# Value products of two key tiles in one run, the compressed branch's weighted probabilities ahead of its block scores, and the last query tile's finishing pieces spread

## The chip, the core and the metric

The kernel runs on one core of a Trainium2 chip. A time is the device time in microseconds (us) of one execution, and the measure is the median of several executions. A core has five engines that each work their own queue of instructions in order and meet through semaphores: TensorE (PE, matmuls; PEld is its weight load), VectorE (DVE), ScalarE (ACT), GpSimd (POOL) and SyncE (SP, which here only issues DMAs).

## What is computed

One layer of a hybrid decoder on 1024 positions of width 1024. A normalized input goes through one projection; half of its columns feed sparse attention (8 heads of 64, 2 key heads), the other half a recurrence; both are concatenated, projected by w_out, added to the input and normalized. The attention part, which the change touches, is this:

```python
s_cmp = jnp.einsum('bgrsd,bgcd->bgrsc', qh, k_cmp) * SCALE
p_cmp = masked_softmax(s_cmp, cmp_end[None, :] <= pos[:, None])
o_cmp = jnp.einsum('bgrsc,bgcd->bgrsd', p_cmp, v_cmp.astype(f32))
imp = jnp.einsum('bgrsc,cj->bgsj', p_cmp, cmp_to_sel_matrix(n_cmp, n_sel))
...
_, sel_idx = lax.top_k(imp, top_n)            # 8 blocks of 64 keys for each query
...
p_sel = masked_softmax(s_sel, (k_pos <= tq[:, None])[:, :, None])   # over the chosen blocks
o_sel = jnp.einsum('bgrqm,bgqmd->bgrqd', p_sel, v_g.astype(f32))
...
p_win = masked_softmax(s_win, w_mask)         # over a window of 512 keys
o_win = jnp.einsum('bgrqk,bgkd->bgrqd', p_win, vwc.astype(f32))
...
o = g[..., 0:1] * o_cmp + g[..., 1:2] * unblock(o_sel) + g[..., 2:3] * unblock(o_win)
...
return x + mix @ w_out
```

## The kernel before

The program goes through a projection stage, the recurrence woven into it, and from about 650 us the attention stage, which alone the change touches (one instance of its first part, for query tile 5, is done at the end of the projection stage). There the 1024 queries are eight tiles of 128, taken in the order 1, 5, 4, 3, 6, 2, 7, 0. Each tile has two branches: b = 0, the selected blocks, and b = 1, the window. A branch runs over key tiles of 128 (`nk` of them: i + 1 for b = 0, at most 5 for b = 1; 66 in all). The chosen blocks are not gathered; a mask in the second operand `q2` excludes the others.

- `Branch.scores(kt)`: PE makes the scores of one key tile, transposed, into `pst` (two PSUM buffers, one for each key head), ACT takes the exponential into `prob` (L1042, three buffers).
- `Branch.values(kt)`: PE multiplies `prob` with the values into `po`. A key tile gives two matmul instructions of 64 output columns, which run as four passes ("po x4" in the trace). Then POOL adds `prob` into `acc` (L1055), for the sum of the softmax; ACT copies `po` to `pos` after the last key tile.
- `Branch.finish()`: PE transposes `acc` (`pz`, L1067), DVE reduces it to sums (L1069), inverts and weights them (`rr`, L1073), POOL widens `rr` to 512 columns (`wide`, L1077), PE transposes that (`prt`, L1081), DVE applies it to `pos`.
- `compressed()`: the compressed blocks of the tile after this one: scores `pcs`, DVE and ACT the softmax (L909, exponential L910, multiplication by the inverse sum L919), the block scores `sp` (L922) and the choice of 8, the gate-weighted probabilities `pw` (L945, "pc" in the trace as well), their transposes on PE (`pct`, L950), ACT's copy (L953), and PE's product with the compressed values, `poc`.
- `row_max()`: an upper bound of the scores from products `pd` and `ps` on PE and reductions on DVE (`bm`, L982 and L994; `nm`, L1006); PE transposes the result (`pnm`, L1008), DVE writes it into `q2` (L1009), which the scores need.
- `load_w_out()`: eight pieces of w_out, each loaded by SP to `wor` (two buffers, which the `xt` tiles of the output share), split by ACT into `woh` (L1113) and by POOL into the remainder `wol` (L1114). Four are left for the branch of tile 5, b = 0.
- `output()`: w_out's product `pout` for a finished query tile, in pieces of three matmuls.

PE's order is fixed by the order of the code. DVE, ACT, POOL and SP are ordered by a scheduler that simulates the program, and then work their queues in that order. `run` walks a branch's key tiles and lets a `Side` object emit pieces of other generators at set fractions of the branch; `side.at` places the finishing pieces of the branch before, at steps 1.2, 1.6 and 3.0 of `nk`, and at 0.95 at the latest. `late_values` keeps the value products one key tile behind the scores.

## Time and profile before

| what | value |
|---|---|
| median of three executions | 1052.12 us (1043.89 to 1053.36) |
| profiled execution, its span | 1040.26 us, 1038.5 us |
| busy PE, PEld, DVE, ACT, POOL | 930.2, 658.6, 584.0, 335.5, 448.2 us |
| mean granted TensorE clock | 0.951 |
| PE busy in 650 to 1039 us, the attention stage | 341.55 of 389 us |

The span goes from the first instruction to the last of the profiled execution; 1.8 us lie around it. The busy times overlap. The granted clock is a share of the full 2.4 GHz; a stretch at 0.5 is one at 1.2 GHz. The last row is the sum of five stretches (80.72, 96.68, 90.73, 45.61 and 27.81 us).

### The profile page before, as it was taken

What the parts mean: (1) busy time and instruction counts of PE and PEld (TensorE: products, weight loads), DVE (VectorE), ACT (ScalarE), POOL (GpSimd) and SP (SyncE); (2) the same over time, 40 slices, a digit from 0 to 9 for tenths busy, and PEclk for the clock granted to TensorE, in tenths of its full rate; (3) what the DMA queues carried; (4) which work ended last, traced back from release to release, by engine and by line L of the source; (5) the groups of instructions that cost most, each with busy time, mean ns of one, the idle gap of its engine ahead of it and who ended that gap; (6) DMA issues with size and microseconds to landing.
All of it is one profiled execution on the core that took longest, in us unless ns stands there. A gap on an engine that the chain in (4) does not pass through costs nothing.

```text
span 1038.5 us, 17087 instructions
## 1 busy us (share of the span) xinstructions
PE 930.2 (90%) x6353; PEld 658.6 (63%) x6353; DVE 584.0 (56%) x1245; ACT 335.5 (32%) x650; POOL 448.2 (43%) x732
## 2 busy tenths in 40 slices
PE   5999999989998999899669978689999999889976
PEld 4888777766676766677458756354565656455555
DVE  7533545555575657374424335677659856685544
ACT  5533233224233443243121212433333333224321
POOL 3100153466483847444521120577463555246521
PEclk9999999999999999799889988879999999899989
DMA  7433453424426453536476293741132312231121
GB/s 259 125 102 102 125 157 108 130 76 116 135 76 172 134 154 119 131 106 170 116 218 192 65 203 95 212 122 31 41 63 79 77 46 69 53 80 33 39 84 41
DMA packets 154429, 115.66 MB, mean 111 GB/s; under 512 B 54369, under 2 KB 132266, under 8 KB 154346
## 3 DMA queue, kind: packets, MB, share of 16 engines
q1 hardware_dynamic: 154346, 114.57, 40.3%
q8 instruction: 50, 0.82, 0.3%
q14 instruction: 33, 0.27, 0.1%
HBM read 76.19 MB, written 35.19 MB: 107 GB/s over the span
## 4 chain that ended last, share of the span: by engine, by line
PE 60%; DVE 10%; DMA 9%; POOL 7%; SPq 6%; issue 5%; ACT 2%; POOLq 0%; DVEq 0%; ACTq 0%
PE pout L113 7%; SPq L85 6%; PE pst L113 6%; PE po L113 5%; PE p_r L113 4%; PE p_k L113 3%; PE p_gn L113 3%; PE p_gr L113 3%; PE p_q L113 3%; PE pc L113 2%; POOL lt L586 2%; POOL ltmp L584 2%; PE ps L113 2%; PE pd L113 2%; PE pcm L113 2%
## 5 line engine op out<-in xcount | busy, mean ns | idle before, releaser
L584 POOL TENSOR_TENSOR ltmp<-la,lt 128x60 f32<-128x60 f32 (+24 forms) x248 | 83.7, 337 | 65.3 <-DMA la<-dA 42.7
L1042 ACT ACTIVATE prob<-pst 128x512 f32<-128x512 f32 x132 | 74.6, 593 | 109.9 <-PE pst L113 106.3
L1055 POOL TENSOR_TENSOR acc<-acc,prob 128x1024 f32<-128x1024 f32 x36 | 86.7, 2409 | 45.1 <-ACT prob L1042 44.9
L586 POOL TENSOR_TENSOR lt<-lt,ltmp 128x60 f32<-128x60 f32 (+24 forms) x248 | 87.6, 353 | 18.8
L113 PE MATMUL pst<-q,k 128*128 128x512 f32 (+1 forms) x264 | 82.3, 430 | 0.0
L994 DVE TENSOR_REDUCE bm<-ps 128x6 f32<-128x384 f32 (+1 forms) x106 | 63.5, 613 | 26.6 <-PE ps L113 26.0
L113 PE MATMUL po<-prob,vt 128*64 128x512 f32 x264 | 75.1, 648 | 0.0
L1055 POOL TENSOR_TENSOR acc<-prob 128x1024 f32<-128x1024 f32 x14 | 33.7, 2410 | 82.6 <-ACT prob L1042 82.6
L113 PEld LDWEIGHTS pst<-q,k 128*128 128x128 f32 (+1 forms) x264 | 48.9, 196 | 14.9 <-issue 5.7
L113 PE MATMUL pout<-woh,mh 128*128 128x512 f32 x128 | 57.6, 450 | 0.2 <-DVE xt L1153 0.2
L113 PE MATMUL ps<-k,q 128*128 128x384 f32 (+3 forms) x136 | 45.4, 386 | 7.7 <-DVE bm L994 3.7
L113 PE MATMUL pout<-wol,mh 128*128 128x512 f32 x128 | 51.3, 401 | 0.0
L113 PE MATMUL pout<-woh,ml 128*128 128x512 f32 x128 | 51.2, 400 | 0.0
L113 PEld LDWEIGHTS ps<-k,q 128*128 128x128 f32 x136 | 25.6, 205 | 35.2 <-DVE bm L994 14.3
L982 DVE TENSOR_REDUCE bm<-pd 128x8 f32<-128x512 f32 x40 | 27.4, 688 | 26.2 <-PE pd L113 26.0
L113 PEld LDWEIGHTS pout<-woh,mh 128*128 128x128 f32 x128 | 25.1, 196 | 20.7 <-issue 17.8
L683 ACT ACTIVATE x<-pc 64x128 f32<-64x128 f32 x32 | 8.7, 272 | 75.4 <-DVE x L682 75.2
L113 PE MATMUL pd<-k,q 128*128 128x128 f32 x160 | 31.1, 321 | 2.1 <-POOL k L868 2.1
L1077 POOL TENSOR_TENSOR wide<-rr,ones 128x512 f32<-128x512 f32 x16 | 17.1, 1068 | 36.1 <-DVE rr L1073 34.1
L1069 DVE TENSOR_REDUCE zz<-pz 128x4 f32<-128x512 f32 x32 | 21.8, 684 | 13.4 <-PE pz L1067 13.0
L1153 DVE TENSOR_TENSOR xt<-pout,xt 128x512 f32<-128x512 f32 x16 | 11.1, 691 | 32.4 <-PE pout L113 32.4
L113 PEld LDWEIGHTS pd<-k,q 128*128 128x128 f32 x160 | 25.9, 204 | 4.0 <-POOL k L868 2.4
(518 smaller groups left out, 2447.7 us busy)
## 6 DMA issues: line engine op xcount, KB each, us to landing
dM<-mix SPq DMA_DIRECT2D x24, 256.0 KB
q<-dQH SPq DMA_DIRECT2D x22, 256.0 KB
la<-dA SPq DMA_DIRECT2D x32, 128.0 KB
xt<-in_x_dram SPq DMA_DIRECT2D x8, 512.0 KB
out_dram<-xt SPq DMA_DIRECT2D x16, 256.0 KB
x<-in_x_dram SPq DMA_DIRECT2D x7, 512.0 KB
mixk<-dM SPq DMA_DIRECT2D x8, 256.0 KB
mixr<-dM SPq DMA_DIRECT2D x8, 256.0 KB
```

The lines of the kernel that those rows point to most:

```text
L85: return nc.sync.dma_start(plain(o), plain(i))
L113: return T.matmul(o, l, r, start=start, stop=stop)
L584: G.tensor_tensor(tv, la[:, j:j + 1, j + 1:].to_broadcast([128, m, n]), lt[:, :m, j:j + 1].to_broadcast([128, m, n]), op=OP.mult)
L586: G.tensor_tensor(lt[:, :m, j + 1:], lt[:, :m, j + 1:], tv, op=OP.add)
L683: gate["A"] = A.activation(x1[1][HP[1], c:8:4, :], pv[HP[1], :, 64:128], AF.Copy)
L982: V.tensor_reduce(bm[:, g * 4:g * 4 + 4, j:j + 2], p.rearrange("p (r b c) -> p r b c", b=2, c=64), axis=AX.X, op=OP.max)
L994: V.tensor_reduce(bm[:, h0:h0 + n, j:j + 2 * w], p[:, :n * w * 128].rearrange("p (h b c) -> p h b c", h=n, c=64), axis=AX.X, op=OP.max)
L1042: A.activation(pr[:, g * 512:(g + 1) * 512], p, AF.Exp)
L1055: G.tensor_tensor(s, self.acc, pr, op=OP.add)
L1069: V.tensor_reduce(zz[:, g, :], p.rearrange("p (r k) -> p r k", r=4), axis=AX.X, op=OP.add)
L1077: G.tensor_tensor(wide, rr.rearrange("p r g -> p (r g)").unsqueeze(2).to_broadcast([128, 8, 64]), ones64.unsqueeze(1).to_broadcast([128, 8 ...
L1153: V.tensor_tensor(xt[:, hs], p, xt[:, hs], op=OP.add)
```

## The change

There are three edits.

1. `run` lets three key tiles' values become pending and then emits two of them in one run; what is left of a branch is emitted after the first scores of the next branch. The 66 value runs on PE become 38: 28 merges. The addition into `acc` moves from `values` to `scores`, so that POOL has it right behind the exponential.
2. In `compressed()` the product `pw` and its transposes `pct` come ahead of the block scores `sp` and the choice of 8 (this concerns tiles 4 to 7 of the queries).
3. For a branch with one key tile (tile 0, the last) the finishing pieces of the branch before come at 0.61, 0.61 and 0.95 of the branch, and the `pout` pieces begin at 0.3 instead of 0.

```diff
@@ compressed
         pw = h2("pc", 2, (128, 4, 2, 64))
         if i >= 4:
             V.tensor_tensor(pe, pe, z8.unsqueeze(2).to_broadcast([128, 8, 64]), op=OP.mult)
+            pg = gv
+        else:
+            pg = sm.tile([128, 8], FT, tag="pg", name="pg")
+            V.tensor_tensor(pg, gv, z8, op=OP.mult)
+        V.tensor_tensor(pw.rearrange("p r g c -> p g r c"), pe.rearrange("p (g r) c -> p g r c", g=2),
+                        pg.rearrange("p (g r) -> p g r", g=2).unsqueeze(3)
+                        .to_broadcast([128, 2, 4, 64]), op=OP.mult)
+        p = psM("pct")
+        for r in range(4):
+            T.transpose(p[:, r * 128:(r + 1) * 128], pw[:, r].rearrange("p g c -> p (g c)"), ident)
+        if i >= 4:
             sp = sm.tile([128, 2, 68], FT, tag="sp", name="sp")
...
-            pg = gv
-        else:
-            pg = sm.tile([128, 8], FT, tag="pg", name="pg")
-            V.tensor_tensor(pg, gv, z8, op=OP.mult)
-        V.tensor_tensor(pw.rearrange("p r g c -> p g r c"), pe.rearrange("p (g r) c -> p g r c", g=2),
-                        pg.rearrange("p (g r) -> p g r", g=2).unsqueeze(3)
-                        .to_broadcast([128, 2, 4, 64]), op=OP.mult)
-        p = psM("pct")
-        for r in range(4):
-            T.transpose(p[:, r * 128:(r + 1) * 128], pw[:, r].rearrange("p g c -> p (g c)"), ident)
         yield
@@ Branch.scores
                 A.activation(pr[:, g * 512:(g + 1) * 512], p, AF.Exp)
+            if kt == 0:
+                self.acc = pr
+            else:
+                s = a2("acc", 2, (128, 1024)) if kt == 1 else self.acc
+                G.tensor_tensor(s, self.acc, pr, op=OP.add)
+                self.acc = s
@@ Branch.values: the same six lines go
@@ the attention stage
+    def flush(keep):
+        while len(late_values) > keep:
+            u, k = late_values.pop(0)
+            u.values(k)
     def run(br, side):
         for kt in range(br.nk):
             br.scores(kt)
+            side.emit((kt + 0.6) / br.nk)
+            if kt == 0:
+                flush(0)
             late_values.append((br, kt))
-            side.emit((kt + 0.6) / br.nk)
-            if len(late_values) > 1:
-                u, k = late_values.pop(0)
-                u.values(k)
+            if len(late_values) == 3:
+                flush(1)
             side.emit((kt + 1) / br.nk)
...
-                    side.at(before.finish(), (1.2, 1.6, 3.0), br.nk)
+                    side.at(before.finish(), (1.2, 1.6, 3.0) if br.nk > 1 else (0.61, 0.61, 0.95), br.nk)
...
-                    side.add(outs[n - 2], 8)
+                    side.add(outs[n - 2], 8, 0.0 if br.nk > 1 else 0.3)
...
-        u, k = late_values.pop(0)
-        u.values(k)
+        flush(0)
```

How the order changes is shown at three places. The first is PE at the first tile, between its window branch and the scores and bounds of what follows; the number behind x counts matmul instructions, two for a key tile's values. The difference, with + for the changed kernel:

```order
 L113 LDWEIGHTS identb
 L113 MATMUL pst<-maskb,identb 128x512
-L113 MATMUL po<-prob,vt_6553 64x512 x2
 L113 MATMUL pst<-q_6524,k_6538 128x512
 L113 MATMUL pst<-q_6529,k_6541 128x512
@@ -2416,5 +2415,5 @@
 L113 MATMUL pd<-k_6532,q_6546 128x128 x4
 L113 MATMUL ps<-k_6532,q_6546 128x512 x3
-L113 MATMUL po<-prob,vt_6553 64x512 x2
+L113 MATMUL po<-prob,vt_6553 64x512 x4
```

The first key tile's value product has moved behind the next scores and stands beside the second's.

The second place is the branch of tile 5, b = 0, where the last four pieces of w_out are split. `prob_7110`, `prob_7145` (7144 after) and `prob_7225` (7226) are its key tiles 1, 2 and 3, `pc_7172` (7173) is the exponential of tile 4's compressed scores, `pc_7264<-pct` the copy of their transposes. ACT before:

```order
L1059 ACTIVATE pos_7089<-po_7036 128x512
L1113 ACTIVATE woh_7342<-wor_7339 128x1024
L1042 ACTIVATE prob_7110<-pst_7111 128x512
L1042 ACTIVATE prob_7110<-pst_7115 128x512
L910 ACTIVATE pc_7172<-pc_7172 128x512
L1113 ACTIVATE woh_7383<-wor_7380 128x1024
L1042 ACTIVATE prob_7145<-pst_7146 128x512
L1042 ACTIVATE prob_7145<-pst_7150 128x512
L1113 ACTIVATE woh_7437<-wor_7434 128x1024
L953 ACTIVATE pc_7264<-pct_7200 128x512
```

And ACT after:

```order
L1114 ACTIVATE woh_7342<-wor_7339 128x1024
L1043 ACTIVATE prob_7060<-pst_7065 128x512
L1114 ACTIVATE woh_7382<-wor_7379 128x1024
L1060 ACTIVATE pos_7089<-po_7084 128x512
L1114 ACTIVATE woh_7439<-wor_7436 128x1024
L1043 ACTIVATE prob_7110<-pst_7111 128x512
L1043 ACTIVATE prob_7110<-pst_7115 128x512
L910 ACTIVATE pc_7173<-pc_7173 128x512
L1114 ACTIVATE woh_7467<-wor_7464 128x1024
L1043 ACTIVATE prob_7144<-pst_7145 128x512
L1043 ACTIVATE prob_7144<-pst_7149 128x512
L954 ACTIVATE pc_7264<-pct_7182 128x512
```

The third of the four pieces (7437 before, 7439 after) has moved from behind key tile 2's exponentials to ahead of key tile 1's. POOL in the same branch before:

```order
L1114 TENSOR_TENSOR wol_7343<-wor_7339,woh_7342 128x1024
L1055 TENSOR_TENSOR acc_7168<-prob_7061,prob_7110 128x1024
L1114 TENSOR_TENSOR wol_7384<-wor_7380,woh_7383 128x1024
L1077 TENSOR_TENSOR wide_7211<-rr_7208,ones64_6514 128x512
L1055 TENSOR_TENSOR acc_7168<-acc_7168,prob_7145 128x1024
L1114 TENSOR_TENSOR wol_7438<-wor_7434,woh_7437 128x1024
```

And POOL after:

```order
L1115 TENSOR_TENSOR wol_7343<-wor_7339,woh_7342 128x1024
L1115 TENSOR_TENSOR wol_7383<-wor_7379,woh_7382 128x1024
L1115 TENSOR_TENSOR wol_7440<-wor_7436,woh_7439 128x1024
L1048 TENSOR_TENSOR acc_7119<-prob_7060,prob_7110 128x1024
L1115 TENSOR_TENSOR wol_7468<-wor_7464,woh_7467 128x1024
L1048 TENSOR_TENSOR acc_7119<-acc_7119,prob_7144 128x1024
L1078 TENSOR_TENSOR wide_7212<-rr_7209,ones64_6514 128x512
```

`wide` stood behind one addition and now stands behind two and the last piece of w_out. In four other branches (tile 5 b = 1, tile 4 b = 1, tile 6 b = 0, tile 7 b = 0) `wide` has likewise moved behind the addition of key tile 2.

The third place is PE at the end, where tile 0's selected branch is finished. Before:

```order
L113 MATMUL pout_9676<-woh_7467,mh_8933 128x512
L113 MATMUL pout_9676<-woh_7467,ml_8934 128x512
L113 MATMUL pout_9676<-wol_7468,mh_8933 128x512
L1067 MATMUL pz_9731<-ident_69,prob_9559 128x128 x4
L1067 MATMUL pz_9737<-ident_69,prob_9559 128x128 x4
L1081 MATMUL prt_9748<-ident_69,wide_9746 128x128 x4
L113 MATMUL po_9756<-prob_9665,vt1_6555 64x512 x2
```

And after:

```order
L1068 MATMUL pz_9695<-ident_69,prob_9560 128x128 x4
L1068 MATMUL pz_9701<-ident_69,prob_9560 128x128 x4
L113 MATMUL pout_9676<-woh_7342,mh_8934 128x512
L113 MATMUL pout_9676<-woh_7342,ml_8935 128x512
L113 MATMUL pout_9676<-wol_7343,mh_8934 128x512
L113 MATMUL pout_9676<-woh_7382,mh_8934 128x512
L113 MATMUL pout_9676<-woh_7382,ml_8935 128x512
L113 MATMUL pout_9676<-wol_7383,mh_8934 128x512
L113 MATMUL pout_9676<-woh_7439,mh_8934 128x512
L113 MATMUL pout_9676<-woh_7439,ml_8935 128x512
L113 MATMUL pout_9676<-wol_7440,mh_8934 128x512
L1082 MATMUL prt_9721<-ident_69,wide_9719 128x128 x4
```

Nine `pout` matmuls now stand between the `pz` transposes and `prt`, and three more behind it, ahead of the value product. At the finish of the branch before (tile 7, b = 1) `pnm` and nine `pout` matmuls stand between `pz` and `prt` in the same way, where nothing stood.

## Rows read from the trace of the kernel before

**Rows 1.** Windows, core 0: us, busy (count) per engine, PE clock, DMA share, GB/s

```profile
960.00:985.00 25.00, 25.00 (x117) 15.18 (x117) 11.88 (x26) 8.62 (x16) 13.38 (x8) 1.00 0.10 32
```

**Rows 2.** The page's chain of work that ended last, by engine

```profile
PE 60%; DVE 10%; DMA 9%; POOL 7%; SPq 6%; issue 5%; ACT 2%; POOLq 0%; DVEq 0%; ACTq 0%
```

**Rows 3.** Windows at a low granted clock, columns as in rows 1

```profile
693.00:701.00 8.00, 5.26 (x17) 3.97 (x19) 7.79 (x19) 2.42 (x4) 5.39 (x3) 0.57 0.40 109
...
885.00:892.00 7.00, 5.75 (x18) 3.53 (x19) 4.12 (x18) 0.60 (x1) 1.04 (x1) 0.51 0.17 65
1001.00:1008.00 7.00, 5.79 (x15) 3.30 (x16) 3.23 (x8) 1.32 (x2) 2.33 (x2) 0.51 0.26 84
```

**Rows 4.** Tile po in 650 to 1039 us: duration ns min/median/max

```profile
L113 PE MATMUL po<-prob,vt x264: 592/643/1117, 651.2 to 1004.2; 128*64 128x512 f32 x132
```

**Rows 5.** Timeline of PE around one value run: start, us, instructions

```profile
863.07 0.40 PE L113 MATMUL ps<-k,q 128*128 128x256 f32 x2
863.40 1.08 PE L113 MATMUL po<-prob,vt 128*64 128x512 f32 x4
864.41 0.50 PE L113 MATMUL pout<-woh,mh 128*128 128x512 f32 x1
864.74 0.39 PE L113 MATMUL pout<-woh,ml 128*128 128x512 f32 x1
864.97 0.39 PE L113 MATMUL pout<-wol,mh 128*128 128x512 f32 x1
```

**Rows 6.** The same run in a narrower window, which cuts its groups

```profile
863.19 0.28 PE L113 MATMUL ps<-k,q 128*128 128x256 f32 x1
863.40 0.65 PE L113 MATMUL po<-prob,vt 128*64 128x512 f32 x2
```

**Rows 7.** Timeline of PE where a value run follows the compressed product

```profile
703.07 1.08 PE L113 MATMUL poc<-pc,vc 64*64 64x512 f32 x4
704.08 1.08 PE L113 MATMUL po<-prob,vt 128*64 128x512 f32 x4
```

**Rows 8.** Timeline at pct of tile 6, and of tile 7; [idle before, releaser]

```profile
788.59 0.63 PE L950 MATMUL pct<-ident,pc 128*128 128x128 f32 x4 [2.15 <-DVE rr L1073]
...
884.58 1.02 DVE L922 TENSOR_REDUCE sp<-pc 128x128 f32<-128x512 f32 x1
...
886.25 1.12 PE L950 MATMUL pct<-ident,pc 128*128 128x128 f32 x4 [4.06 <-DVE pc L945]
```

**Rows 9.** Timeline in tile 5's selected branch, four engines

```profile
685.22 1.08 ACT L1042 ACTIVATE prob<-pst 128x512 f32<-128x512 f32 x2 [1.62 <-PE pst L113]
...
686.07 6.21 SPq L85 DMA_DIRECT2D wor<-in_w_out_dram  x4
...
690.97 1.06 ACT L1113 ACTIVATE woh<-wor 128x1024 fp32r<-128x1024 f32 x1 [0.83 <-DMA wor<-in_w_out_dram]
...
695.74 1.12 PE L950 MATMUL pct<-ident,pc 128*128 128x128 f32 x4 [4.89 <-DVE pc L945]
...
696.97 1.06 PE L1081 MATMUL prt<-ident,wide 128*128 128x128 f32 x4
...
706.82 0.32 PE L1008 MATMUL pnm<-ident,nm 128*104 128x128 f32 x1 [1.67 <-DVE nm L1006]
```

**Rows 10.** Timeline from one set of scores to prt, tile 4's selected branch

```profile
738.18 1.09 PE L113 MATMUL pst<-q,k 128*128 128x512 f32 x4
738.91 1.09 ACT L1042 ACTIVATE prob<-pst 128x512 f32<-128x512 f32 x2 [3.29 <-PE pst L113]
...
740.14 2.37 POOL L1055 TENSOR_TENSOR acc<-acc,prob 128x1024 f32<-128x1024 f32 x1 [2.09 <-ACT prob L1042]
...
743.56 0.66 PE L1081 MATMUL prt<-ident,wide 128*128 128x128 f32 x4 [0.52 <-POOL wide L1077]
```

**Rows 11.** Timeline of PE at the two finishes of the last tile

```profile
988.76 0.66 PE L1081 MATMUL prt<-ident,wide 128*128 128x128 f32 x4 [2.80 <-POOL wide L1077]
...
1002.21 1.12 PE L1081 MATMUL prt<-ident,wide 128*128 128x128 f32 x4 [3.80 <-POOL wide L1077]
```

More of the change, by code (lines that the diff above doesn't have):

```diff
@@ L1050, in values @@
                    pr[:, g * 512:(g + 1) * 512], start=(kt == 0), stop=(kt == self.nk - 1))
-            if kt == 0:
-                self.acc = pr
-            else:
-                s = a2("acc", 2, (128, 1024)) if kt == 1 else self.acc
-                G.tensor_tensor(s, self.acc, pr, op=OP.add)
-                self.acc = s
             if kt == self.nk - 1:
```

## The prediction

> **What bounds the kernel now.** I read the windows of the attention stage first, since the change touches nothing else but one piece of the projection stage. Where the stage runs well, PE is busy without a gap and at the full clock, 25.00 of 25.00 us [rows 1], and the chain of waits that ended last lies on PE for 60% [rows 2]. There, only PE time that is taken away counts. Three other stretches look different: PE is busy only in part, and what it does it does near half speed, at a granted clock of 0.57, 0.51 and 0.51, so mostly at 1.2 of 2.4 GHz [rows 3]. The reader is to see that each of them has a wait of PE in it or ahead of it, 4.89, 4.06 and 3.80 us [rows 8, 9, 11]. There the other engines set the time, and what their queues hold is what counts. So the first edit is priced by PE's steps and the others by waits.
>
> The sum is made against the profiled execution, 1040.26 us. It lies 1.1% under the median of the three, 1052.12 us; the result is scaled by that ratio at the end. The three executions differ by 0.9%, and about 1% (10.5 us) is what a measurement of this kernel can tell from no change.
>
> **Edit 1, value runs.** What a lone run costs is read from matmul starts. The second `ps` starts 0.12 us after the first (863.19 against 863.07), and the run begins 0.21 after it, at 863.40 [rows 5, 6]: 0.09 for the way in. The four passes end at 864.48; the last has at least 0.59 [rows 4], so the second pair began at 863.88, 0.48 after the first. The engine goes on at 864.41, 0.53 after the second pair. The first `pout` matmul then holds it for 0.33 and the second for 0.23 [rows 5]: another 0.10. Together 0.09 + 0.48 + 0.53 + 0.10 = 1.20 us. Two key tiles in one run, if they go on at the step of 0.48, cost 0.09 + 3 x 0.48 + 0.53 + 0.10 = 2.16, which is 0.24 less than 2.40. The nearest row for a boundary inside such a run is the compressed product followed by a value run: 1.01 us from start to start, 0.48 + 0.53 [rows 7], which would save 0.19. 28 merges give 5.3 to 6.7 us. Four lie in tile 5's selected branch, which is priced apart below, and about six of the other 24 end in a wait of PE on DVE or POOL, as the run ahead of `pct` of tile 6 does [rows 8], where PE only comes earlier. 18 x 0.24 = 4.3; I take **-4.2**, with -3.4 (18 x 0.19) and -6.7 (28 x 0.24) as ends.
>
> The trace shows that a second pass follows the first at 0.48 us with its weight load hidden [rows 5, 6]. In a sentence of its own: the Trainium skill, "TensorE: Matmul & The Clock Gate" (section "The mechanism"), says a weight load overlaps running matmuls only where the row group differs; a key tile's values take all rows, so by that the second tile of a run would wait for its loads, and the gain would nearly vanish. By its "TensorEngine Tiling (Array Packing)" (section "Key Properties") only a change of tiling mode drains the engine, which a run of two does once instead of twice. No run here has yet shown two such tiles side by side; the first is rival C.
>
> The merge takes away cover too. A set of scores keeps its two PSUM buffers until the exponentials have read them: the first is free some 0.73 + 0.55 us after the scores start (738.18 to 738.91, and half of 1.09) [rows 10], say 1.3, and the scores themselves take four steps of 0.23, 0.95. So 0.35 us of other work must stand between two sets. Before it was always a value run; now for 28 of them it is only what `Side` has, a `pout` piece of 0.7 us (three steps of 0.23 [rows 5]), which covers it, or a pair of `ps`, 0.24, which doesn't quite. At 0.05 each I take **+1.5**; the ends are 0 and +4 (28 x 0.14).
>
> **The additions in the new place.** Issued behind the exponential, an addition stands earlier in POOL's queue, and in four branches `wide` is now behind that of key tile 2. From scores to `prt` the chain of exponential, addition and `wide` is 743.56 - 738.18 = 5.38 us [rows 10]. Counted from the changed order at the steps of rows 5, PE has 3.6, 4.9, 4.2 and 4.2 us of work of its own between those scores and its `prt`: waits of 1.75, 0.5, 1.2 and 1.2. At 743.56 PE's own work becomes 5.45 and the 0.52 of before goes. Behind the waiting `prt` stands all of PE's queue, so they count in full: **+4.1**. If the merged run stands ahead of the wait, part is cover: 0 as the one end; +4.7 as the other.
>
> **Edit 2.** The reduction of `sp`, 1.02 us, stood between the multiplication and `pw` on DVE [rows 8]; it is now behind. At tile 7 PE waited for just this, 4.06 us: -1.0. At tile 6 PE waited 2.15 us, but the value run ahead of `pct` has gone into a later one, so PE arrives 1.08 us earlier and finds `pct` 1.0 earlier: 0. Tile 5's `pct` lies in the projection stage amid other matmuls: 0. Tile 4's is in the next part. What is late next is the mask: `sp` and the choice of 8 come 0.7 us later (`pw` [rows 8] now precedes them), and `pnm` needs them; it stands far enough behind. **-1.0**, ends 0 and -3.
>
> **Tile 5's selected branch.** Here the queues are dealt anew. ACT's third piece of w_out now stands ahead of key tile 1's exponentials, and before ACT waited for just this piece's load: SP issued it at 686.07, when POOL had freed the buffer, and ACT had it at 690.97, 4.9 us later [rows 9]. The two pieces ahead of it can start some 2 us sooner, so I put the issue at 684, the piece at 689 to 690, and the exponentials at 689.9 instead of 685.22: 4.7 us late. Behind them in ACT's queue are tile 4's exponential and so `pct`; PE's `pct`, which already waited 4.89, comes some 2.5 later even with `sp` out of the way. On POOL the piece and two additions of 2.4 to 2.8 us now precede `wide`: `prt` at about 701.1 instead of 696.97, +4.1. Not all of it stays: further on PE waited 1.67 us for `nm` [rows 9], which DVE can have done in the meantime; with that and four merges (1.0) partly spent, I take **+2.7**. The ends are 0 (the load comes sooner, and the waits of before only change places) and +7.5 (the exponentials' delay in full and a longer stretch at the low clock, of which the one of before cost 5.26 x 0.43 = 2.3 us [rows 3]).
>
> **Edit 3.** Nine `pout` matmuls at 0.23, 2.1 us, go into each of two waits, of 2.80 and 3.80 us [rows 11]. In the first the write of `q2` comes into DVE's queue between the sums: 1.5 stays. In the second, DVE had the addition of the finished `pout` half, its norm and the root between the sums; with the last piece behind `prt` they come later, and 0.4 stays. 6.60 - 1.9 = 4.7. The low clock of 1001 to 1008 costs 5.79 x 0.49 = 2.8 us [rows 3] and followed that wait; a stretch of 0.57 also came where PE had waited only 2.15 [rows 8], so I count on 1.8 of it. **-6.5**; the ends are -3.3 (half of the waits and nothing of the clock) and -7.6.
>
> **The sum**: -4.2 + 1.5 + 4.1 - 1.0 + 2.7 - 6.5 = **-3.4 us**, 1036.9 on the profiled execution, and 1052.12 x 1036.9 / 1040.26 = 1048.7 on the median.
>
> **Rivals.** A, the order holds nobody up: POOL and ACT keep pace in their new orders, the waits at `wide` and in tile 5's branch fill with the merged runs, and the three low stretches go. Then -6.7 (all merges), -2.0 (`pct` of tiles 4 and 7), -5.1 (2.3 + 2.8, clock), -7.6, and +1.5: -19.9 us, or 1032. For it: each low stretch lies at a wait that an edit is aimed at. Against: the changed order puts more of POOL's work ahead of `wide` at five places.
>
> B, slower: in-order queues. ACT's load-bound piece and POOL's additions hold the exponentials and `wide`, and PE's whole queue behind them; the value runs that filled such gaps are gone. +7.5, +4.7, +4.0, one more low stretch +2.5, against -3.4 and -3.3: +12.0 us, or 1064.3. It decides from the point where these waits, which I price at 8.3, exceed the 11.7 us that the other terms give. For it: ACT already waited 0.83 us for that load, and POOL was busy nearly without a pause there. Against: most of the four `wide` waits have over 4 us of matmuls ahead of them.
>
> C, the merge doesn't do what it says: each key tile in a run pays for its own loads, 0.10 [rows 5] ahead of each of two pairs, so that 0.04 of 0.24 is left. Edit 1 gives -0.7 instead of -4.2: +0.1 us, 1052.2. For it: no row shows two key tiles in one run. Against: the 1.01 of rows 7.
>
> **How the numbers follow.** The forecast has 0.46, A 0.25, B 0.16, C 0.13. The forecast's own range, from the ends of its terms that can hold together, is 1041 to 1056. Faster by over 1% (under 1041.6) is most of A and a tail of the forecast: 0.27. Slower by over 1% (above 1062.6) is two thirds of B: 0.11. The rest, 0.62, is within 1%. The range takes in A down to 1031 and B up to 1061.
>
> **What would show it.** In the trace of the changed kernel: four matmul pairs 0.48 apart in a run, 8 passes in about 2.05 us, show edit 1 right, a step of 0.6 or more at the boundary shows C. Waits of `prt` on `wide` at four places of about 1 us, and the last two waits under 2 us, show my prices. In tile 5's branch, key tile 1's exponentials ready soon after the scores would refute the term there, and with no stretch under 0.6 of the clock behind 690 us A holds. The prediction is wrong above all if POOL's order costs nothing, or if a wait that I did not see stands at the start of a branch, where the leftover value run now comes after the next scores.

## The result, and the profile after

The changed kernel took 1051.24 us (median of 20 executions, 1041.52 to 1056.54), the kernel before 1045.61 us in its 20 (1038.14 to 1053.36). The ratio is 1.0062, with a 95% interval of 1.0041 to 1.0084: slower by 0.6%, where 0.3% faster was forecast.

What comes ahead of the attention stage varies from run to run: the stage's first exponential started at 640.2 us in the profiled execution before, at 647.9 after, and anywhere from 637.0 to 649.6 in the others. Within the stage, a branch whose work is not changed takes nearly the same time in every trace (tile 7, b = 1: 19.89 in the kernel before and in the three runs that merge nothing); only the branches of tile 1, b = 1, and tile 5, b = 0, trade up to 0.7 us with each other (23.89 and 33.67 before, 24.52 and 32.96 in a run that differs from it at the end alone), and their sum stays. So traces are compared by the start of each branch's first exponential (its first `prob<-pst` on ACT), up to the next branch's, in three parts, in us:

| part | before | after | difference |
|---|---|---|---|
| tile 1, b = 1 | 23.89 | 26.48 | +2.59 |
| tile 5, b = 0 | 33.67 | 36.88 | +3.21 |
| tile 5, b = 1 | 16.95 | 25.16 | +8.21 |
| these three, "the stretch" | 74.51 | 88.53 | +14.02 |
| tile 4, b = 0, to tile 7, b = 1, "the middle" | 248.82 | 248.87 | +0.05 |
| tile 0 to the last instruction, "the end" | 62.15 | 55.12 | -7.03 |

The three parts give +7.0 us. Ahead of them tile 1's first branch is shorter by 0.9 (11.89, 12.83 before), so the stage is 6.1 us longer; the ratio makes it 6.5 (0.0062 x 1045.61). The loss is all in the stretch. For its three branches the forecast had nothing, +2.7 (the term for tile 5's selected branch, four merges in it) and +1.75 (the wait of `prt` in the next).

In the timeline of the changed kernel from tile 5's selected branch on, four engines (times are to be lowered by 6.8 us, 659.80 - 652.99, to stand beside rows 9):

```profile
680.34 2.35 POOL L1115 TENSOR_TENSOR wol<-wor,woh 128x1024 fp32r<-128x1024 f32 x1
682.80 1.42 POOL L1078 TENSOR_TENSOR wide<-rr,ones 128x512 f32<-128x512 f32 x1
684.27 1.12 PE L1082 MATMUL prt<-ident,wide 128*128 128x128 f32 x4 [3.47 <-POOL wide L1078]
...
697.08 1.06 ACT L1114 ACTIVATE woh<-wor 128x1024 fp32r<-128x1024 f32 x1 [4.35 <-DMA wor<-in_w_out_dram]
698.04 1.07 ACT L1043 ACTIVATE prob<-pst 128x512 f32<-128x512 f32 x2
698.67 2.07 PE L113 MATMUL pst<-q,k 128*128 128x512 f32 x4 [3.32 <-ACT prob L1043]
...
709.55 1.12 PE L1082 MATMUL prt<-ident,wide 128*128 128x128 f32 x4 [2.38 <-POOL wide L1078]
720.34 0.32 PE L1009 MATMUL pnm<-ident,nm 128*104 128x128 f32 x1
```

The scores of key tile 1 were done, but their exponentials waited in ACT's queue behind a piece of w_out, and that for its load, 4.35 us; the next scores then waited 3.32 us for PSUM that the exponentials had not read. A new wait of PE stands where before PE had gone straight through, and `prt` waits for `wide`, which before [rows 9] it did not. Ahead of all this, in tile 1's second branch, `wide` stood behind another piece of w_out on POOL, and `prt` waited 3.47 us.

The next branch, tile 5, b = 1, in the same kernel's timeline, POOL, DVE and PE:

```profile
732.35 2.35 POOL L1048 TENSOR_TENSOR acc<-acc,prob 128x1024 f32<-128x1024 f32 x1 [0.94 <-ACT prob L1043]
732.51 2.25 DVE L1005 TENSOR_TENSOR bm<-bm,nm 128x40 f32<-128x40 f32 x1
734.68 0.16 DVE L1074 TENSOR_TENSOR rr<-zz,gt 128x8 f32<-128x8 f32 x1
...
734.98 1.04 POOL L1078 TENSOR_TENSOR wide<-rr,ones 128x512 f32<-128x512 f32 x1 [0.28 <-DVE rr L1074]
...
736.08 1.11 PE L1082 MATMUL prt<-ident,wide 128*128 128x128 f32 x4 [2.02 <-POOL wide L1078]
...
739.67 2.34 POOL L1048 TENSOR_TENSOR acc<-acc,prob 128x1024 f32<-128x1024 f32 x1 [0.33 <-ACT prob L1043]
740.69 1.38 DVE L1005 TENSOR_TENSOR bm<-bm,nm 128x40 f32<-128x40 f32 x1
...
742.40 0.32 PE L1009 MATMUL pnm<-ident,nm 128*104 128x128 f32 x1 [2.71 <-DVE nm L1007]
```

Before the change, the same instructions of DVE and POOL:

```profile
718.75 0.16 DVE L1073 TENSOR_TENSOR rr<-zz,gt 128x8 f32<-128x8 f32 x1
...
719.05 1.04 POOL L1077 TENSOR_TENSOR wide<-rr,ones 128x512 f32<-128x512 f32 x1 [1.12 <-DVE rr L1073]
719.42 0.72 DVE L1004 TENSOR_TENSOR bm<-bm,nm 128x40 f32<-128x40 f32 x1
720.05 2.39 POOL L1055 TENSOR_TENSOR acc<-acc,prob 128x1024 f32<-128x1024 f32 x1
```

The reader is to see the second line of the first fence: an addition over 40 columns took 2.25 us on VectorE, and it ended at 734.76, when POOL's addition ended at 734.70. `rr` stood behind it, `wide` behind `rr`, and `prt` waited. But POOL itself had been busy with key tile 2's addition until 734.70, so an earlier `rr` would have let `wide` start only 0.28 us sooner: most of this wait comes from the addition's place ahead of `wide` in POOL's queue. A second addition of VectorE, 1.38 us, again ended just behind POOL's (742.07 and 742.01), and `nm` and `pnm` stood behind it.

This is one of the four places where `wide` had moved behind key tile 2's addition. At the other three `prt` waited as well:

```profile
790.89 0.66 PE L1082 MATMUL prt<-ident,wide 128*128 128x128 f32 x4 [0.48 <-POOL wide L1078]
...
859.85 0.66 PE L1082 MATMUL prt<-ident,wide 128*128 128x128 f32 x4 [1.80 <-POOL wide L1078]
...
960.13 0.66 PE L1082 MATMUL prt<-ident,wide 128*128 128x128 f32 x4 [1.14 <-POOL wide L1078]
```

Windows behind two of the waits above, and one around the later wait of rows 11, now at 1018.09, columns as in rows 1:

```profile
709.00:719.00 10.00, 9.02 (x24) 5.08 (x26) 7.94 (x20) 3.56 (x6) 5.22 (x3) 0.50 0.00 0
736.00:740.00 4.00, 3.61 (x10) 2.56 (x10) 1.33 (x3) 1.19 (x2) 1.62 (x3) 0.57 0.00 0
1015.00:1022.00 7.00, 6.49 (x32) 4.27 (x31) 4.78 (x8) 2.47 (x5) 3.68 (x4) 1.00 0.00 1
```

After the waits at 709.55 and 736.08 PE worked mostly at 1.2 GHz, as it did in rows 3; before, the clock was 1.00 throughout 707 to 750:

```profile
707.00:750.00 43.00, 40.06 (x195) 23.11 (x195) 27.93 (x47) 14.56 (x26) 23.99 (x12) 1.00 0.18 43
```

At the end the two waits of rows 11 are now 1.18 and 0.51 us, and the low clock that stood behind the second, 1001 to 1008 before, is gone:

```profile
1007.89 0.66 PE L1082 MATMUL prt<-ident,wide 128*128 128x128 f32 x4 [1.18 <-POOL wide L1078]
...
1018.09 0.65 PE L1082 MATMUL prt<-ident,wide 128*128 128x128 f32 x4 [0.51 <-POOL wide L1078]
```

The merged run itself, PE's timeline (to be held against rows 5):

```profile
724.93 1.94 PE L113 MATMUL po<-prob,vt 128*64 128x512 f32 x8
726.80 0.50 PE L113 MATMUL ps<-k,q 128*128 128x512 f32 x1
```

Two key tiles take 726.80 - 724.93 = 1.87 us, one takes 1.01 [rows 5].

### The profile page after: what moved, and what is told of

Same layout as the page of the kernel before. It is cut to its first block, busy times and chain, and to the rows that moved or that the text cites. A ratio compares the mean times of both kernels' runs of the same rounds, so it can differ in the third digit from the quotient of the medians.

```text
span 1052.3 us, 17083 instructions
## 1 busy us (share of the span) xinstructions
PE 933.2 (89%) x6353; PEld 666.2 (63%) x6353; DVE 584.1 (56%) x1245; ACT 335.5 (32%) x650; POOL 445.3 (42%) x732
## 4 chain that ended last, share of the span: by engine, by line
PE 58%; DMA 11%; DVE 9%; POOL 8%; issue 6%; SPq 5%; ACT 2%; POOLq 0%; ACTq 0%; DVEq 0%
PE pst L113 6%; PE pout L113 6%; SPq L85 5%; PE po L113 5%; PE p_r L113 4%; PE p_k L113 3%; PE p_gr L113 3%; PE pc L113 2%; POOL ltmp L584 2%; PE p_v L113 2%; POOL lt L586 2%; PE p_kc L113 2%; PE p_gn L113 2%; PE p_q L113 2%; PE pcm L113 2%
## 5 line engine op out<-in xcount | busy, mean ns | idle before, releaser
L113 PE MATMUL pst<-q,k 128*128 128x512 f32 (+1 forms) x264 | 87.0, 449 | 3.4 <-ACT prob L1043 3.3
L113 PE MATMUL po<-prob,vt 128*64 128x512 f32 x264 | 69.3, 642 | 0.0
L113 PEld LDWEIGHTS pst<-q,k 128*128 128x128 f32 (+1 forms) x264 | 51.6, 207 | 16.1 <-ACT prob L1043 4.6
L113 PEld LDWEIGHTS po<-prob,vt 128*64 128x64 f32 x264 | 16.5, 144 | 30.4 <-issue 29.4
L113 PEld LDWEIGHTS pout<-wol,mh 128*128 128x128 f32 x128 | 24.2, 189 | 5.5
```

Source lines behind the costliest of these rows:

```text
L113: return T.matmul(o, l, r, start=start, stop=stop)
```

## The experiments

Four theories were held against each other. Theory 1: exponentials wait in ACT's queue behind pieces of w_out that wait for their load, and `wide` behind the other half of these pieces on POOL. Theory 2: the additions' new place makes `wide` late. Theory 3: PE lacks the cover of the lone value runs. Theory 4, formed after the first runs: VectorE's small instructions with two operands in SBUF stand still while POOL's run, and both the merge and the edit on the compressed branch shifted them into POOL's work. All ratios are to the kernel before on the same chip, with 95% intervals; the first table's parts are given as stretch, middle and end.

**w_out in order.** By the code the last four pieces belong to tile 5's second branch; the scheduler had drawn them into the first. They are kept in the code's order:

```diff
-            A.activation(h_, raw, AF.Copy)
-            G.tensor_tensor(l_, raw, h_.bitcast(FT), op=OP.subtract)
+            tc.keep_in_program_order(A.activation(h_, raw, AF.Copy))
+            tc.keep_in_program_order(G.tensor_tensor(l_, raw, h_.bitcast(FT), op=OP.subtract))
```

> The changed kernel with the splitting of w_out (ACT's and POOL's instruction of each of the eight pieces) kept in the order in which the code emits it, so that no piece can stand ahead of the exponentials written before it. Measured by the stretch from the first exponential of tile 1, b = 1, to the first of tile 4, b = 0: 74.5 us in the kernel before, 88.5 in the changed one. Theory 1 (the exponentials of tile 5 wait in ACT's queue behind pieces whose load has not landed, and additions and wide in POOL's behind the other half): the stretch comes back to 73 to 78 us, exponentials within 1 us of their scores, and the ratio to the kernel before is 0.990 to 0.996. Theory 2 (the additions' new place, and their collision with DVE, make wide and the bounds late): the stretch stays over 83 us and the ratio over 1.001. Theory 3 (the merged value runs leave PE uncovered between score sets): the same as theory 2, with waits of PE on exponentials.

Measured: 0.9961 (0.9927 to 0.9995); stretch 78.14, middle 248.76, end 55.12. Of 14.0 us 10.4 are back: 3.9 in tile 1's branch, 4.9 in tile 5's first, but only 1.6 in its second, which still took 23.61. The first two are now shorter than before the change, by 1.3 and 1.7 us, for the run also moves work: of the eight pieces on POOL none is left in tile 1's branch; three lie in tile 5's first, four in its second, one behind it. The exponentials now follow their scores:

```profile
686.03 1.05 ACT L1114 ACTIVATE woh<-wor 128x1024 fp32r<-128x1024 f32 x1
687.87 1.08 ACT L1043 ACTIVATE prob<-pst 128x512 f32<-128x512 f32 x2 [0.79 <-PE pst L113]
```

Theory 1 holds for the first two branches, as far as ACT's and POOL's pieces together go; they were not moved apart, and what their order cost is not told apart from what the branches save without them.

**The additions back in `values`.** The six lines move back from `scores`; nothing else.

> The changed kernel with the addition into acc back in values, behind the value products. ACT's order in tile 5's selected branch is that of the changed kernel. Theory 1: the stretch of 88.5 us stays within 85 to 91, ratio to the kernel before 1.004 to 1.010. Theory 2: the stretch falls under 81 us, ratio 0.996 or less.

Measured: 1.0011 (0.9980 to 1.0042); stretch 88.31, middle 248.96, end 55.13. Every branch is within 0.3 us of the changed kernel's, though the ratio of the whole came out lower than the expected 1.004; the varying time ahead of the stage may be why, which is not shown. The place in the code doesn't matter, because the scheduler puts the addition in the same place of POOL's queue. So this run doesn't test what that place in the queue costs; a later one does.

**The spread finish alone.** The two lines of edit 3 in the kernel before.

> The kernel before with the last tile's finishing pieces spread, and nothing else. All theories: the stretch from the first exponential of tile 0, b = 0, to the end, 62.2 us before and 55.1 in the changed kernel, is 54.5 to 56.5 here, and the ratio to the kernel before 0.992 to 0.995. If it is above 0.998, part of what the end gains is given back elsewhere.

Measured: 0.9916 (0.9890 to 0.9941); stretch 74.45, middle 248.59, end 55.11. The end gains 7.0 us and nothing is given back; the ratio is just under the expected 0.992.

**The merge alone.** Edit 1 in the kernel before.

> The kernel before with the merged value runs and the additions behind the exponentials, and nothing else. Theories 1 to 3 alike: the loss is this edit's, the stretch of tiles 1 and 5 is 86 to 92 us, and the ratio to the kernel before 1.011 to 1.016 (the changed kernel's 1.006 without the end's gain). If the ratio is under 1.008, the edit on the compressed branch carries part of the loss.

Measured: 1.0103 (1.0064 to 1.0142); stretch 84.73, middle 249.37, end 62.19. The stretch and the ratio lie just under what was expected (86 and 1.011), the ratio over 1.008: the merge carries most of the loss, 10.2 us of the stretch's 14.0. The other 3.8 come with edit 2.

**Additions pinned as well.** The kernel with w_out in order, and the additions back in `values` and pinned too, to put `wide` ahead of key tile 2's addition in tile 5's second branch. (By its trace it stood there already with w_out in order alone, 724.89 and 725.89; what stood right ahead of it was a piece of w_out.)

```diff
-                G.tensor_tensor(s, self.acc, pr, op=OP.add)
+                tc.keep_in_program_order(G.tensor_tensor(s, self.acc, pr, op=OP.add))
```

> The changed kernel with the splitting of w_out in the order of the code, and the additions into acc back in values and kept in the order of the code too, so that wide of tile 5, b = 1, stands ahead of key tile 2's addition on POOL, as before the change; at tile 4, b = 1, it still stands behind. In the kernel with w_out in order alone that branch of tile 5 took 23.6 us from its first exponential to the next branch's (16.95 before the change). If wide's place on POOL is what made it late: 16.5 to 18.5 us, tile 4, b = 1, stays at 22.2 (21.06 before), and the ratio to the kernel before is 0.987 to 0.992. If it is the merged run itself, with less cover for PE, or the low clock left over from the branch before: 22 us or more, and the ratio stays at about 0.996.

Measured: 1.0124 (1.0089 to 1.0159); stretch 81.78, middle 262.43, end 55.23; tile 5, b = 1, 27.44. The expectation missed what else the pin does: an addition now waits for the value run in whose lines it stands, and the next finish for the addition:

```profile
718.86 0.66 PE L1068 MATMUL pz<-ident,acc 128*128 128x128 f32 x4 [2.62 <-POOL acc L1056]
```

A wait of `pz` came in beside that of `prt` (1.21 us, 2.79 with w_out in order), so this run doesn't tell the causes apart. The middle is 13.6 us longer than the changed kernel's.

**Merging from tile 4 on.** For tiles 1 and 5 the values of one key tile at a time:

```diff
         for kt in range(br.nk):
             br.scores(kt)
+            if br.L["n"] < 2:
+                late_values.append((br, kt))
+                side.emit((kt + 0.6) / br.nk)
+                flush(1)
+                side.emit((kt + 1) / br.nk)
+                continue
```

> The changed kernel, but for query tiles 1 and 5 the values of one key tile at a time, as before; the additions stay behind the exponentials, edits 2 and 3 stay. If merging alone re-deals the queues there: the stretch of tiles 1 and 5 is 73 to 76 us (74.5 before, 88.5 in the changed kernel), the middle (first exponential of tile 4, b = 0, to that of tile 0, b = 0) 248.5 to 249.5 as in both kernels, and the ratio to the kernel before 0.991 to 0.995. If the additions' place is a cause of its own, the stretch is over 80 us.

Measured: 0.9917 (0.9880 to 0.9954); stretch 77.02, middle 246.02, end 55.12. The tile 5, b = 1, branch is at 16.97, as before the change, so its loss of 8.2 us comes with the merge there. The stretch is 1 us over the expectation, and what is left of the loss is in tile 5's first branch, 35.76 (33.67 before).

The middle is 2.5 us under the expectation, 2.9 under the changed kernel's. That difference lies in tile 2's two branches, 46.74 and 50.73 us, though PE, ACT and POOL have the same order there in both. As windows, this run's and the changed kernel's:

```profile
883.83:930.57 46.74, 39.10 (x191) 24.54 (x189) 37.05 (x80) 13.87 (x28) 14.07 (x8) 1.00 0.32 77
896.11:946.84 50.73, 43.20 (x191) 26.89 (x189) 37.98 (x80) 13.87 (x29) 14.08 (x8) 0.90 0.28 70
```

In both `pct` waits 3.13 us for `pc`; behind this wait the clock fell in the one and not in the other. So a difference of up to 4 us in the middle, between single traces, says little of an edit.

**No merge.** Edits 2 and 3 in the kernel before.

> The kernel before with the edit on the compressed branch and the spread finish, without the merge. The end takes 54.5 to 56.0 us as in the run of the finish alone. If the compressed branch's edit is worth the 1 us that was predicted: stretch of tiles 1 and 5 73 to 75 us, middle 247 to 248.5, ratio 0.990 to 0.9935. If it costs time at tile 5 (the run of the merge alone had a stretch of 84.7, the changed kernel 88.5): stretch 77 us or more, ratio over 0.995.

Measured: 0.9905 (0.9866 to 0.9943); stretch 77.06, middle 249.20, end 55.12. Beside the finish alone (74.45) edit 2 costs 2.6 us in the stretch, all of it in tile 5's first branch (35.53 against 32.96): the second outcome, though the ratio is that of the first. PE waits less for `pct`, 3.25 us instead of 4.89 [rows 9] (6.17 with the finish alone), and then 5.99 for bounds. The timeline there, PE, DVE and POOL:

```profile
694.61 2.81 POOL L1056 TENSOR_TENSOR acc<-acc,prob 128x1024 f32<-128x1024 f32 x1
697.38 2.36 POOL L1115 TENSOR_TENSOR wol<-wor,woh 128x1024 fp32r<-128x1024 f32 x1
699.70 2.34 POOL L1056 TENSOR_TENSOR acc<-acc,prob 128x1024 f32<-128x1024 f32 x1
702.00 2.34 POOL L1115 TENSOR_TENSOR wol<-wor,woh 128x1024 fp32r<-128x1024 f32 x1
...
696.38 1.11 DVE L940 TENSOR_TENSOR imh<-sp 128x32 f32<-128x32 f32 x1
697.41 0.55 DVE L995 TENSOR_REDUCE bm<-ps 128x6 f32<-128x384 f32 x1
697.88 1.91 DVE L941 SCALAR_TENSOR_TENSOR im<-imh,im 128x32 f32<-128x32 f32 x1
699.82 2.27 DVE L942 TENSOR_TENSOR im<-im,keep 128x32 f32<-128x32 f32 x1
...
702.68 1.77 DVE L950 TENSOR_SCALAR nm<-sl 128x16 f32<-128x16 f32 x2
...
706.35 0.69 PE L113 MATMUL ps<-k,q 128*128 128x384 f32 x1 [5.99 <-DVE bm L995]
```

Each of the four lines over 16 or 32 columns ends some 0.1 us behind an instruction of POOL: 697.49 (697.42), 699.79 (699.74), 702.09 (702.04), 704.45 (704.34). The reduction between them, which reads PSUM, took its usual 0.55. POOL worked without a pause, so each of them waited for one of POOL's. It is the rule and not the exception: in the trace of the changed kernel from 640 us on, VectorE has 36 such small instructions with two inputs in SBUF (`bm`, `rr`, `imh`, `im`). The 22 that began while none of POOL's TENSOR_TENSOR instructions ran took at most 0.22 us; of the other 14, 13 ended within 0.1 us after POOL's, and took up to 2.37 us; the last one began together with POOL's and took 0.16. The Trainium skill, "SBUF — State Buffer" (section "Who interferes with whom"), has the rule: VectorE and GpSimd share one pair of ports, an exclusive lock held for a whole instruction, which VectorE needs for two SBUF inputs. These rows agree; by that page the fourth, with one input, contends only in a 2-port performance mode, which no row names.

**The addition behind `wide` again.** In the four branches key tile 2's addition is queued behind `wide` on POOL, by an order of issue alone:

```diff
+            elif kt == 2 and (i, b) in WIDE_FIRST:
+                self.held = pr
+            elif kt == 3 and (i, b) in WIDE_FIRST:
+                with tc.issue_after(last_wide[0].ins):
+                    G.tensor_tensor(self.acc, self.acc, self.held, op=OP.add)
+                    G.tensor_tensor(self.acc, self.acc, pr, op=OP.add)
```

> The changed kernel, with one thing else: in the four branches where wide has moved behind key tile 2's addition on POOL (tile 5 b = 1, tile 4 b = 1, tile 6 b = 0, tile 7 b = 0) that addition is queued behind wide again; PE's order is the changed kernel's. Theory 4 (VectorE's instructions with two operands in SBUF stand still while POOL's addition runs, so rr and the masked bounds come late at tile 5, b = 1, wide behind them, and PE's waits end in the low clock): that branch falls from 25.2 us to 17 to 20, the bounds' addition takes under 0.8 us instead of 2.25, tile 4, b = 1, from 22.2 to 21 to 21.5, and the ratio to the kernel before is 0.998 to 1.003 (1.006 for the changed kernel). Rival (PE lacks the cover of the lone value runs): the branch stays at 23 us or more, and PE waits for exponentials or bounds elsewhere in it.

Measured: 1.0030 (1.0006 to 1.0054); stretch 84.13, middle 251.13, end 55.13; tile 5, b = 1, 20.71 (25.16), tile 4, b = 1, 21.56 (22.25). Lines of DVE, `prt` and `pnm` in that branch:

```profile
730.47 0.19 DVE L1005 TENSOR_TENSOR bm<-bm,nm 128x40 f32<-128x40 f32 x1
730.58 0.17 DVE L1083 TENSOR_TENSOR rr<-zz,gt 128x8 f32<-128x8 f32 x1
...
731.98 0.65 PE L1091 MATMUL prt<-ident,wide 128*128 128x128 f32 x4
...
735.17 0.38 DVE L1005 TENSOR_TENSOR bm<-bm,nm 128x40 f32<-128x40 f32 x1
...
735.88 0.32 PE L1009 MATMUL pnm<-ident,nm 128*104 128x128 f32 x1 [1.84 <-DVE nm L1007]
```

With POOL idle the same addition takes 0.19 us instead of 2.25, and `prt` doesn't wait. The branch ends 0.7 over the expected 20, and 4.45 us are back. But the edit moved two things at once, POOL's addition away from `wide` and away from VectorE's, so the 4.45 are not all the lock's. Counted from the branch's first exponential (723.16 and 721.13), `prt` comes 2.07 us sooner, of which the late `rr` was 0.28 and POOL's own queue the rest; `pnm` comes 2.42 sooner still, of which 1.00 is VectorE's second addition (0.38 instead of 1.38) and 1.4 is that PE is no longer at the low clock there. By these rows the lock has 1.3 of the 4.45; this split is read from rows, and no run shows it. So theory 2, taken as the place in POOL's queue, has the larger share here, and theory 4 the smaller.

Theory 3 falls for these 4.45 us: all merges are kept, and PE waits for no exponential in this branch. The 3.8 us that it still takes beyond 16.95 lie 1.25 ahead of `prt`, where a second key tile of left-over values from the branch before stands (0.86, 1.87 - 1.01), and 2.5 behind `pnm`, where eight passes of a value run took 3.25 us at a granted clock of 0.56, and before the change four took 1.01. Here too no run shows it, and theory 3 isn't excluded. The middle is 2.3 us longer than the changed kernel's: tile 6's first branch took 33.04 us (31.11), though the wait of its `prt` fell from 1.80 to 0.11. So the end of a wait is not yet a gain of its length.

**POOL with less to do.** Edits 2 and 3, and the last four remainders of w_out not computed:

```diff
+            if k < 4:
+                l_ = wo_l[k + 4]
+            else:
+                G.tensor_tensor(l_, raw, h_.bitcast(FT), op=OP.subtract)
```

> The kernel before with the edits on the compressed branch and on the finish, and with POOL spared the remainders of w_out's last four pieces (the other four's are used in their place, so this part of the product is left out). In the run with those two edits PE waited 5.99 us for bounds at tile 5, b = 0, behind a choice of blocks whose small instructions took 1.1 to 2.3 us each. Theory 4: those instructions fall to 0.2 to 0.3 us, with one exception at most, the wait to under 2 us, and the stretch of tiles 1 and 5 from 77.1 us to 70 to 73.5. Rival (the choice is simply later in VectorE's queue, its length is its own): the instructions keep their length, the wait stays over 4 us, the stretch over 75.

Measured: 0.9895 (0.9845 to 0.9945); stretch 71.89, middle 246.88, end 55.16. DVE's timeline, and POOL's:

```profile
694.91 4.80 POOL L1056 TENSOR_TENSOR acc<-acc,prob 128x1024 f32<-128x1024 f32 x2 [3.17 <-ACT prob L1043]
...
694.56 0.21 DVE L940 TENSOR_TENSOR imh<-sp 128x32 f32<-128x32 f32 x1
...
695.15 2.20 DVE L941 SCALAR_TENSOR_TENSOR im<-imh,im 128x32 f32<-128x32 f32 x1
...
697.87 1.90 DVE L942 TENSOR_TENSOR im<-im,keep 128x32 f32<-128x32 f32 x1
...
702.73 0.23 DVE L950 TENSOR_SCALAR nm<-sl 128x16 f32<-128x16 f32 x2
```

Two of the four are short, the two that fell into the pair of additions are not, and the wait for bounds is 3.90 us, not under 2: the size was expected too large, but that VectorE's small instructions wait for POOL's is shown line by line. The stretch is 5.2 us shorter, as expected. The loads of w_out also come sooner here, so not all of that is the lock's.

**The mix.** Merging from tile 4 on, and in `compressed()` the old order for tile 4 alone, whose choice of blocks falls into tile 5's first branch:

```diff
+        if i != 4:
+            V.tensor_tensor(pw.rearrange("p r g c -> p g r c"), pe.rearrange("p (g r) c -> p g r c", g=2),
...
         if i >= 4:
             sp = sm.tile([128, 2, 68], FT, tag="sp", name="sp")
...
+        if i == 4:
+            V.tensor_tensor(pw.rearrange("p r g c -> p g r c"), pe.rearrange("p (g r) c -> p g r c", g=2),
...
         yield
```

> The changed kernel with one key tile's values at a time for query tiles 1 and 5, and the old order in the compressed branch for tile 4 alone (tiles 5, 6 and 7 keep the new one). By theories 1 and 4 both losses are then gone: the stretch of tiles 1 and 5 is 74 to 75.5 us, the middle 245.5 to 247, the end 55, and the ratio to the kernel before 0.987 to 0.991, the lowest of all. If the old order at tile 4 only moves the wait, the stretch stays at 77 and the ratio at 0.992.

Measured: 0.9905 (0.9871 to 0.9940); stretch 74.32, middle 244.85, end 55.15. The stretch is that of before, the middle the shortest of all runs of the whole computation. It is faster than both kernels, but the interval doesn't set it apart from the spread finish alone (0.9916).

**Both repairs, all merges kept.** w_out in order and the addition behind `wide`; then the same with the old order for tile 4.

> Both single repairs together: the changed kernel with the splitting of w_out in the order of the code and, in the four branches, key tile 2's addition behind wide. Each alone left a stretch of tiles 1 and 5 of 78.1 and of 84.1 us. If the two causes are separate, the stretch is 72 to 76 us and the ratio to the kernel before 0.990 to 0.995. If the pieces of w_out, which now lie in tile 5's second branch, hold wide there in the addition's place, that branch stays over 21 us and the stretch over 76.

> The same, and in the compressed branch the old order for tile 4 alone. If the new order costs time there only as long as POOL is busy with w_out, which is now elsewhere, the stretch differs from the run before by less than 1 us; if it costs in itself, it is 1.5 to 3 us shorter. Ratio to the kernel before 0.988 to 0.995.

Measured: 0.9985 (0.9959 to 1.0011), stretch 80.84, middle 249.90, end 55.13; and 0.9957 (0.9926 to 0.9988), stretch 78.77, middle 249.46, end 55.13. Both ratios, and the first stretch, are above what separate causes would have given (0.995, 76). The first went the second way: tile 5, b = 1, took 25.51, for the pieces of w_out lie there now, and one stands right ahead of `wide`:

```profile
715.81 2.34 POOL L1124 TENSOR_TENSOR wol<-wor,woh 128x1024 fp32r<-128x1024 f32 x1
718.33 1.04 POOL L1087 TENSOR_TENSOR wide<-rr,ones 128x512 f32<-128x512 f32 x1 [0.17 <-DVE rr L1083]
```

The second is shorter by 2.1 us, 1.9 of them in tile 5's first branch: edit 2 costs that at tile 4 even with fewer pieces of w_out beside it (three on POOL in that branch, five before).

## Why the prediction was wrong

**The step that failed** is in "The additions in the new place": the waits of `prt` "count in full", +4.1, so a wait of PE is worth its own length and no more. The waits themselves were priced well: 1.75, 0.5, 1.2 and 1.2 us forecast, 2.02, 0.48, 1.80 and 1.14 measured. But the branch of the first, tile 5, b = 1, lost 8.21. From the branch's first exponential `prt` came 3.32 us later than before, `pnm` another 2.43, and the next branch yet another 2.46. The sum had nothing for what made it so: the low clock behind the wait (0.57 at 736 to 740), the addition that VectorE could not do beside POOL's, and the left-over run of two key tiles at the low clock. With key tile 2's addition behind `wide` again, 4.45 of the 8.21 came back; the other 3.8 stay open. Nor had the sum a term for tile 1's second branch, where a piece of w_out held `wide`: +2.59.

**Tile 5's selected branch** was priced at +2.7, ends 0 and +7.5, and took 3.21 more. The chain in it was right: on the clock of rows 9 the exponentials came at 698.04 - 6.81 = 691.2 (689.9 forecast), `prt` at 702.7 (701.1). That these times agree so well is in part luck, since 2.6 of both delays came from the branch ahead. "Not all of it stays" was right as well, PE's wait of 1.67 us for `nm` is gone; 709 to 719 at the low clock cost instead. What failed was to let the effect of the pieces of w_out end with this branch: with them in order 10.4 us of the stretch came back, 5.5 of them in its two neighbours.

**The duration of small instructions** was a premise that wasn't stated. The prediction took each instruction of DVE at its length in the trace of before and moved it. The lock that makes a 0.2 us addition last 2.25 was not weighed, though that trace had it (1.98 us for `rr` at 689.19 while POOL split w_out). By the rows it is 1.3 us in tile 5's second branch, and it lengthens the choice of blocks ahead of the 5.99 us wait that edit 2 brought at tile 4.

**Edit 2.** At tile 7 the wait fell from 4.06 to 3.13 us (-1.0 forecast), at tile 6 it is 2.43 (no gain forecast against 2.15): as waits, both right.

```profile
811.93 0.63 PE L929 MATMUL pct<-ident,pc 128*128 128x128 f32 x4 [2.43 <-DVE pc L924]
...
907.92 1.11 PE L929 MATMUL pct<-ident,pc 128*128 128x128 f32 x4 [3.13 <-DVE pc L924]
```

Wrong was what would be late next: not the mask but the bounds of the branch's own queries, which stand behind the choice on DVE. That cost 2.6 us at tile 4's, more than all its gains. And with the finish alone beside it, the edit has no gain in the middle either (249.20 against 248.59).

**Edit 1's run** was mis-sized on the good side. Eight passes take 1.87 us, so a merge saves 2 x 1.20 - (0.09 + 1.87 + 0.10) = 0.34, not 0.24; rival C falls: the second key tile's loads didn't hold the run up. The cover that the merge takes away, +1.5, cost nothing in the middle, where the trace has no wait of the scores for an exponential over 0.15 us. For the middle the sum had -1.3 (-4.2, +1.5, -1.0 and the three `wide` waits left of +4.1, 2.4), against +0.05. That this is close is luck: tile 4's first branch took 2.25 us longer and tile 3's first 2.48 less, and tile 2's two took 50.73 with the clock partly low, 46.74 in the run with the same order of PE and the clock at 1.00. So what a merge is worth in the middle isn't shown: 3.2 us by one pair of traces (246.02 against 249.20), which is less than the difference of tile 2's branches in that pair (46.74 and 52.17), and -0.6 by another (249.37 against 248.82). In tile 1's first branch it gave 0.9.

**Edit 3**: -6.5 forecast, -7.0 measured; the low clock behind the wait went altogether, where 1.8 of its 2.8 us was counted on.

**The rivals.** B named the mechanism, ACT's load-bound piece and POOL's additions with PE's queue behind them, and its direction; it had 0.16. It gave +12 us where +6.5 came by the ratio: the stretch lost more than B had for it, but the end gained 7.0, where B left it 3.3, and the middle lost nothing. Rival A falls with the stretch.

## What to carry to other kernels

Where a scheduler orders the engines that a change doesn't touch, read its new order first and price every place where an instruction that waits for a load has moved ahead of one on the path; a delay there is to be followed into the next stages, not to the next wait. A wait of PE can cost several times its length, by the low clock that may follow it and by the work that it pushes into another engine's; two us of it stood in a branch that lost eight. An edit that looks good by PE's steps can be kept where it pays, and left out where the other queues are full: the finish alone, and the mix, were faster by 0.8 and 1.0% than the kernel before. Single traces are to be compared branch by branch, with the granted clock beside each time. VectorE's short instructions with two SBUF operands belong where GpSimd is idle.

## What was not expected of the hardware

A second key tile's passes of a run come closer together than the first's: 1.87 us for eight against 1.01 for four. And an addition of VectorE over 32 columns can take 2.27 us beside GpSimd's (a like one took 0.21 with GpSimd idle), while a reduction from PSUM between two such additions loses nothing. The clock can fall behind a wait of 3.13 us in one run and not in another, with PE's work in the same order.
